# A two-block network on one core: the second mixer's gate panels and attention output projection traced in pieces among its four streams

## The chip, the core and the metric

The kernel runs on one core of a Trainium2 chip. The metric is the device time of one execution in microseconds; the smaller the better. A core has TensorE (PE in the rows, with PEld for its weight loads), VectorE (DVE), ScalarE (ACT), GpSimd (POOL) and SyncE (SP), which only issues DMAs here.

## What is computed

The reference passes a sequence of 512 positions with 1024 channels through two blocks of two layers each. The change touches only the mixer of the second block's layers:

```python
proj = rmsnorm(x, norm_mix_pre) @ w_in
q, k, v, rw, gate_a, gate_b = _split(proj, (ATT_Q, ATT_KV, ATT_KV, RW_SHIFT_COLS, D_MODEL, D_MODEL))
y_att = sliding_window_attention(rope(q), rope(k), v, att_sinks) @ w_o_att
y_rw = rwkv7_time_mix(rw, ...) @ w_o_rw
mixed = sigmoid(gate_a) * y_att + sigmoid(gate_b) * y_rw
x = x + rmsnorm(mixed @ w_out, norm_mix_post)
```

`sliding_window_attention` has 16 query heads of 64 and 4 key heads, a window of 128. `rwkv7_time_mix` is a linear recurrence of 16 heads of 64 with a 64x64 state each.

## The kernel before

Activations lie feature by position: 8 tiles of 128 features x 512 positions. A **panel** is 128 output features of a weight matrix: 8 k tiles of 128x128. Each float32 operand is split into a high and a low part (hi, lo for activations, wh, wl for weights), and each k tile takes three matmuls of 512 columns, at lines L303 to L305 (`mm_k`). `weights` loads half a panel (four k tiles, 256 KB, L286, issued on SP), copies it to wh on ACT (L287) and subtracts to get wl (L288) on the engine that `self.lo_eng` names, VectorE or GpSimd. `proj` makes a whole panel and leaves it in a PSUM bank.

`mixer2` handles the heads in 8 pairs, and has four streams.

- `keys` runs `rw_a` for each pair: the projection of the keys, small matmuls for decay and norm (L1114, L1121, L1133), elementwise work down to the tile bk (L1146, L1147), and then 8 matmuls at L1157. After every second pair `rw_solve` inverts small triangles on VectorE (L1185, L1186).
- `attention` projects keys, values and queries, rotates them (`rope2`, L943 to L947), and goes through 16 blocks of scores (L983) and values (L1012, L1023). Its result od goes to DRAM.
- `preps` runs `rw_prep`: two projections per pair, then the chunk matrices of the scan (from L1236 on, with a sum over heads at L1246).
- `seqs` runs `rw_seq`: 8 steps per pair, each with two small matmuls (L1317) and copies out of PSUM (L1319, L1320), then a normalisation (L1324 to L1333), transposes (L1339, copied out at L1344) and the gating product (L1350, L1351), whose result yd goes to DRAM.

The first two streams make the keys and attention stage, the last two the scan stage. `interleave` walks through the generators of a stage with an estimated clock, `self.now`, and so sets the order in which their instructions are **traced**. A scheduler then orders each engine's instructions by its own estimates: of what is ready, the instruction traced first goes first, and buffers are handed out in the order that results. What was traced later can thus move ahead into a gap if its buffers are free. Each engine then works strictly through its own order, and waits by semaphores.

Beside the streams there is dense work with no recurrence in it: 16 gate panels (two of them made earlier, with the head of the mixer), each followed by a Tanh on ACT (L1424) and a store, and the 8 panels of w_o_att (`att_out`) on the reloaded attention output. Each of these is multiplied by its gate at L1487 and stored as md. Before, both are traced after all four streams. Rings of buffers are named by `self.S`: gates use the weight ring wg (for the later ones wa too) and the banks mg and sc; attention scores use these two banks as well, projections of keys the bank x1, those of attention x2. `att_out` splits its input into the 16 buffers that hold the mixer's input H until the last projection. `mixer2_out`, which comes next, reloads yd and runs the panels of w_o_rw.

Of the kernel before, what the change touches and what calls it, by code (L numbers as in the profile page):

```python
# [212 lines left out]
class Builder:  # L213
# [110 lines left out]
    def proj(self, panel, acts, bank=None):  # L324
        o = self.ps(bank)
        self.mm3(o, panel, acts)
        return o

# [874 lines left out]
    def rw_prep(self, l, i, H, st):  # L1203
# [6 lines left out]
        v = self.shift(self.proj(win[28 + i], H, "x2"), *self.mu_cols(l, 16 + i))  # L1210
        yield 10.4, 1.0
# [172 lines left out]
    def interleave(self, gens, fill=()):  # L1384
# [4 lines left out]
        rest = [[self.now, g, s] for s, g in fill]  # L1389
        while live:  # L1390
            t = next((t for t in live + rest if t[0] <= self.now + 1e-9), None)
            if t is None:
                self.now = min(t[0] for t in live + rest)
                continue
            self.S = t[2]
            try:
                pe, lat = next(t[1])
                self.now += pe
                t[0] = self.now + lat
            except StopIteration:  # L1400
                (live if t in live else rest).remove(t)
# [9 lines left out]
    def mixer2(self, l, H, pre):  # L1411
# [10 lines left out]
        def gate(j):  # L1422
            t = self.T("gt")
            nc.scalar.activation(t, pre[j] if j in pre else self.proj(win[j], H), AF.Tanh, scale=0.5)  # L1424
            nc.scalar.dma_start(sga[j - 38] if j < 46 else sgb[j - 46], t)

        def gates():
            for i in range(8):
                self.S = "G" if i < self.NG else "G2"
                for j in (38 + i, 46 + i):  # L1430
                    if j not in pre:
                        gate(j)
                        yield 5.2, 0.0

        st = [dict() for _ in range(8)]
# [10 lines left out]
        for j in self.HEAD2[3:]:  # L1446
            gate(j)
        self.S = "K"
        self.rw_low(l, H, pre)
        with ExitStack() as es:  # L1450
# [8 lines left out]
            self.interleave([("K", keys((1, 2, 3))), ("A", self.attention(l, H, od, pre[9]))])  # L1459
        with ExitStack() as es:  # L1460
# [20 lines left out]
            def att_out():  # L1481
                Y = self.reload(od)
                for m in range(8):
                    g = self.T("g")
                    nc.sync.dma_start(g, sga[m])
                    o = self.proj(self.I[f"q_w_o_att{l}"][m], Y)
                    nc.vector.scalar_tensor_tensor(out=g, in0=g, scalar=1.0, in1=o, op0=ADD, op1=MUL)  # L1487
                    nc.scalar.dma_start(md[m], g)

            self.lo_eng = nc.vector  # L1490
            self.interleave([("A", seqs()), ("K", preps())])
            self.S = "G"
            for _ in gates():
                pass
            self.S = "M"
            att_out()
# [125 lines left out]
    def ple(self, l, X, pre, out):  # L1622
# [32 lines left out]
    NG = 3  # L1655
# [51 lines left out]
```

## Time and profile before

| | us |
|---|---|
| median of 3 runs | 4038.19 |
| lowest, highest | 4032.23, 4041.36 |
| the profiled execution | 4036.65 |
| its span, first to last instruction | 4034.8 |

Two layers of the second block follow each other; mixer of layer 0 lies between about 1480 and 2200 us of the span, that of layer 1 some 1297 us later. The rows further down are read like this: busy time of an engine is the time in which one of its instructions ran; a granted clock (PEclk) of 1.00 is TensorE's upper level, 2.4 GHz, and 0.5 its lower one, 1.2 GHz, so a mean between them says how much of a stretch was spent at each.

### The profile page before, as it was taken

The numbers are of one execution on the slowest core, as the hardware profiler recorded it, in microseconds if no ns is written. First come the engines' busy times: TensorE is split into PE (matmuls) and PEld (weight loads), VectorE is DVE, ScalarE is ACT, GpSimd is POOL, SyncE is SP. The second block draws the span as 40 slices with busy tenths as digits, with TensorE's granted clock in tenths as the row PEclk, the third lists the DMA queues.
The fourth block names the chain that finished last, engine by engine and source line by source line (L and its number), as shares of the span: only waits on it lengthen the run. The fifth ranks groups of instructions, "written<-read, shape, count | busy, mean of one in ns | idle before, by whom it ended". The sixth has DMA issues, their size and how long they took to land.

```text
span 4034.8 us, 56574 instructions
## 1 busy us (share of the span) xinstructions
PE 3762.3 (93%) x19888; PEld 3117.2 (77%) x19888; DVE 2667.9 (66%) x5595; ACT 1774.9 (44%) x3727; POOL 576.6 (14%) x515
## 2 busy tenths in 40 slices
PE   7998999999999988889999999998888989999998
PEld 6877888888888876657778888896665777888887
DVE  7888444555644567887664676687788775476667
ACT  4433333544433352435553554455344555354444
POOL 0201000110100033222110200014331220020001
PEclk9999999999999998989999999999888999999999
DMA  8466333312333343343227433344334323743334
GB/s 287 153 204 189 97 94 95 94 48 63 100 95 96 91 147 105 97 128 109 91 65 255 124 107 92 99 153 152 96 98 130 110 81 101 234 126 97 94 96 137
DMA packets 316573, 487.34 MB, mean 121 GB/s; under 512 B 79744, under 2 KB 127744, under 8 KB 316160
## 3 DMA queue, kind: packets, MB, share of 16 engines
q1 hardware_dynamic: 240256, 422.82, 34.0%
q10 hardware_dynamic: 76032, 60.90, 4.7%
q8 instruction: 157, 2.57, 0.3%
q14 instruction: 128, 1.05, 0.1%
HBM read 422.72 MB, written 60.88 MB: 120 GB/s over the span
## 4 chain that ended last, share of the span: by engine, by line
PE 55%; DVE 13%; ACT 3%; issue 3%; POOL 1%; DMA 1%; ACTq 0%; SPq 0%; POOLq 0%; DVEq 0%
PE ps L303 15%; PE ps L304 15%; PE ps L305 15%; DVE tm L1185 2%; PE ps L1317 1%; DVE tt L1186 1%; PE ps L1300 1%; PE ps L1157 1%; DVE ro L946 1%; DVE wl L288 1%; PE ps L983 1%; ACT wh L287 1%; PE ps L1023 1%; PE ps L1280 1%; PE ps L1285 1%
## 5 line engine op out<-in xcount | busy, mean ns | idle before, releaser
L303 PE MATMUL ps<-hi,wh 128*128 128x512 f32 (+1 forms) x4384 | 1635.3, 374 | 41.5 <-DVE ro L946 18.1
L305 PE MATMUL ps<-hi,wl 128*128 128x512 f32 (+1 forms) x4384 | 1622.1, 371 | 9.7 <-DVE wl L288 5.2
L304 PE MATMUL ps<-lo,wh 128*128 128x512 f32 (+1 forms) x4384 | 1622.7, 371 | 7.8 <-DVE lo L449 4.6
L287 ACT ACTIVATE wh<-raw 128x512 fp32r<-128x512 f32 (+1 forms) x1158 | 710.1, 620 | 1281.8 <-PE ps L304 1065.7
L288 DVE TENSOR_TENSOR wl<-raw,wh 128x512 fp32r<-128x512 f32 (+1 forms) x1005 | 690.8, 693 | 515.9 <-ACT wh L287 487.1
L303 PEld LDWEIGHTS ps<-hi,wh 128*128 128x128 f32 x4384 | 840.6, 192 | 181.3 <-issue 19.6
L305 PEld LDWEIGHTS ps<-hi,wl 128*128 128x128 f32 x4384 | 841.4, 192 | 143.7 <-DVE wl L288 7.8
L304 PEld LDWEIGHTS ps<-lo,wh 128*128 128x128 f32 x4384 | 842.5, 192 | 138.4 <-DVE lo L449 4.9
L288 POOL TENSOR_TENSOR wl<-raw,wh 128x512 fp32r<-128x512 f32 (+1 forms) x153 | 200.1, 1318 | 1193.2 <-ACT wh L287 1165.2
L1381 POOL TENSOR_TENSOR x<-x,ys 128x256 f32<-128x256 f32 x48 | 43.6, 909 | 862.9 <-DVE ys L1380 793.0
L482 DVE SCALAR_TENSOR_TENSOR ad<-ad,cact 128x1024 f32<-128x1024 f32 x96 | 116.7, 1220 | 29.2 <-DMA ad<-in_ada 29.1
L175 DVE TENSOR_TENSOR acc<-acc,sq 128x256 f32<-128x256 f32 (+1 forms) x175 | 96.1, 552 | 25.2 <-ACT sq L174 23.1
L1157 PE MATMUL ps<-bk,adg 128*128 128x192 f32 x256 | 67.2, 384 | 46.5 <-DVE bk L1147 20.5
L1319 DVE COPY sv<-ps 64x64 f32<-64x64 f32 x224 | 49.5, 221 | 90.4 <-PE ps L1317 87.6
L1185 DVE TENSOR_TENSOR tm<-lu,tt 128x126 f32<-128x126 f32 (+22 forms) x248 | 100.1, 404 | 9.0 <-DMA lu<-ls 4.0
L1580 DVE TENSOR_TENSOR u<-ps,r 128x512 f32<-128x512 f32 x88 | 60.5, 690 | 67.7 <-PE ps L305 67.0
L1317 PEld LDWEIGHTS ps<-sv,add 128*128 128x128 f32 (+1 forms) x512 | 77.9, 189 | 31.9 <-issue 8.8
L1292 POOL TENSOR_SCALAR add<-rdg 64x512 f32<-64x512 f32 x32 | 51.5, 1609 | 351.3 <-DVE add L1301 226.6
L1157 PEld LDWEIGHTS ps<-bk,adg 128*128 128x128 f32 x256 | 47.3, 216 | 64.8 <-issue 34.2
L1317 PE MATMUL ps<-sv,add 128*128 128x64 f32 (+1 forms) x512 | 91.1, 272 | 3.7 <-DVE sv L1319 2.3
L1320 ACT ACTIVATE y<-ps 64x64 f32<-64x64 f32 x256 | 54.7, 216 | 88.7 <-DVE sv L1319 49.5
L1186 DVE TENSOR_TENSOR tt<-tt,tm 128x126 f32<-128x126 f32 (+22 forms) x248 | 80.7, 325 | 3.7
(356 smaller groups left out, 5168.7 us busy)
## 6 DMA issues: line engine op xcount, KB each, us to landing
raw<-in_q_win SPq DMA_DIRECT2D x224, 256.0 KB, 2.9
ad<-in_ada SPq DMA_DIRECT2D x96, 512.0 KB, 4.4
raw<-in_q_w_up SPq DMA_DIRECT2D x184, 256.0 KB, 2.7
raw<-in_win SPq DMA_DIRECT2D x98, 256.0 KB, 3.1
raw<-in_w_val SPq DMA_DIRECT2D x92, 256.0 KB, 2.6
raw<-in_w_gate SPq DMA_DIRECT2D x92, 256.0 KB, 2.8
raw<-in_q_w_down SPq DMA_DIRECT2D x74, 256.0 KB, 2.6
raw<-in_w_down SPq DMA_DIRECT2D x64, 256.0 KB, 2.6
```

Source lines behind the costliest of these rows:

```text
L175: nc.vector.tensor_tensor(out=self.acc[:, cs], in0=self.acc[:, cs], in1=q, op=ADD)
L287: nc.scalar.activation(h, raw, AF.Copy)
L288: self.lo_eng.tensor_tensor(out=l, in0=raw, in1=h.bitcast(F32), op=SUB)
L303: nc.tensor.matmul(o, h, ah, start=k == first, stop=False)
L304: nc.tensor.matmul(o, h, al, start=False, stop=False)
L305: nc.tensor.matmul(o, l, ah, start=False, stop=k == last)
L482: nc.vector.scalar_tensor_tensor(out=raw, in0=raw, scalar=1.0, in1=self.cact, op0=MUL, op1=MUL, accum_out=m)
L1157: nc.tensor.matmul(o, ad[:, c], bk[:, c], start=True, stop=True)
L1185: nc.vector.tensor_tensor(out=t, in0=lc, in1=tt[:, 0:c, j:j + 1].to_broadcast([P, c, n]), op=MUL)
L1186: nc.vector.tensor_tensor(out=tt[:, 0:c, j + 1:32], in0=tt[:, 0:c, j + 1:32], in1=t, op=ADD)
L1317: nc.tensor.matmul(o, add[h][rows, c], c3(sv[h])[rows, c], start=True, stop=True)
L1580: nc.vector.tensor_tensor(out=u, in0=pj(ff), in1=r2, op=MUL)
```

## The change

The gates and `att_out` become one generator, `dense`, that is handed to both calls of `interleave` as `fill`. It yields after each half panel (four k tiles, 12 matmuls). `interleave` keeps a credit: each segment of a stream adds its estimated TensorE time times a share (0.27 in the keys and attention stage, 0.25 in the scan stage), and pieces are traced while the credit is above zero, or when no stream is due. What is left after the streams is traced at the end. The w_o_att part may begin only once pair 7's projections are traced (`st["proj"]`), since it needs H's buffers. While a piece is traced, `lo_eng` is GpSimd. In the first stage the pieces take the banks x2 and x1 in turn, in the second sc and mg; the ring of gate tiles (2) now also holds g of the w_o_att part. Nothing is computed differently.

```diff
+    def pieces(self, panel, acts, out):
+        o, ws = self.ps(), []
+        for k in range(len(acts)):
+            if k % self.WK == 0:
+                ws.append(self.weights(panel[:, k:min(len(acts), k + self.WK)]))
+            self.mm_k(o, ws, acts, k, slice(0, S))
+            if k % self.WK == self.WK - 1 and k < len(acts) - 1:
+                yield 0.68 * self.WK
+        out.append(o)
...
         v = self.shift(self.proj(win[28 + i], H, "x2"), *self.mu_cols(l, 16 + i))
+        st["proj"] = True
         yield 10.4, 1.0
...
+        def piece():
+            nonlocal credit
+            s, g = fill
+            self.S, lo, self.lo_eng = s, self.lo_eng, self.nc.gpsimd
+            pe = next(g, None)
+            self.lo_eng = lo
+            credit -= pe or 0.0
+            self.now += pe or 0.0
+            return pe
+
         while live:
-            t = next((t for t in live + rest if t[0] <= self.now + 1e-9), None)
+            t = next((t for t in live if t[0] <= self.now + 1e-9), None)
             if t is None:
-                self.now = min(t[0] for t in live + rest)
+                if not (fill and piece()):
+                    self.now = min(t[0] for t in live)
                 continue
...
                 t[0] = self.now + lat
+                credit += pe * share
             except StopIteration:
-                (live if t in live else rest).remove(t)
+                live.remove(t)
+            while fill and credit > 0.0 and piece():
+                pass
...
-        def gates():
+        def dense():
             for i in range(8):
-                self.S = "G" if i < self.NG else "G2"
                 for j in (38 + i, 46 + i):
                     if j not in pre:
-                        gate(j)
-                        yield 5.2, 0.0
+                        o = []
+                        yield from self.pieces(win[j], H, o)
+                        gate(j, o[0])
+                        yield 0.68 * self.WK
+            while "proj" not in st[7]:
+                yield 0.0
+            Y = self.reload(od)
+            yield 0.01
+            for m in range(8):
+                g = self.T("g")
+                nc.sync.dma_start(g, sga[m])
+                o = []
+                yield from self.pieces(self.I[f"q_w_o_att{l}"][m], Y, o)
+                nc.vector.scalar_tensor_tensor(out=g, in0=g, scalar=1.0, in1=o[0], op0=ADD, op1=MUL)
+                nc.scalar.dma_start(md[m], g)
+                yield 0.68 * self.WK
...
-            self.interleave([("K", keys((1, 2, 3))), ("A", self.attention(l, H, od, pre[9]))])
+            self.interleave([("K", keys((1, 2, 3))), ("A", self.attention(l, H, od, pre[9]))], ("F", fill), self.SHARE[0])
...
-            self.interleave([("A", seqs()), ("K", preps())])
-            self.S = "G"
-            for _ in gates():
+            self.interleave([("A", seqs()), ("K", preps())], ("F2", fill), self.SHARE[1])
+            self.S = "M"
+            for _ in fill:
                 pass
-            self.S = "M"
-            att_out()
...
+    SHARE = 0.27, 0.25
```

Three places in TensorE's order show what moves. The first is layer 0's keys stage, between the norm of pair 6 (L1133 before, L1144 after) and its first matmul at L1157 (L1168 after). Before:

```order
L1133 MATMUL ps_15362<-c_hsel,sq_15329 128x64 x4
L1023 MATMUL ps_15397<-pt_15388,vt_13534 64x256
L1023 MATMUL ps_15397<-pt_15395,vt_13534 64x256 x2
L1012 MATMUL ps_15438<-ident,sc_15257 128x128
L1012 MATMUL ps_15438<-ident,sc_15260 128x128
L1012 MATMUL ps_15438<-ident,sc_15257 128x128
L1012 MATMUL ps_15438<-ident,sc_15260 128x128
L983 MATMUL ps_15480<-kd_13546,ro_14845 128x256
L983 MATMUL ps_15480<-kd_13546,ro_14890 128x256
L1157 MATMUL ps_15450<-bk_13139,adg 128x192
```

Afterwards, with ps_15708 a gate's bank (its first rows; eight more matmuls of it, two small ones and the next projection stand before L1168):

```order
L1144 MATMUL ps_15462<-c_hsel,sq_15440 128x64 x4
L1023 MATMUL ps_15538<-ident,sc_15065 128x128
L1023 MATMUL ps_15538<-ident,sc_15062 128x128
L1023 MATMUL ps_15538<-ident,sc_15065 128x128
L303 MATMUL ps_15708<-hi_12288,wh_15710 128x512
L304 MATMUL ps_15708<-lo_12289,wh_15710 128x512
L305 MATMUL ps_15708<-hi_12288,wl_15711 128x512
```

A gate's long matmuls now stand where only attention's small ones stood. The second place is layer 0's scan stage, right after pair 7's last projection. Before, with ps_18522 a gate:

```order
L305 MATMUL ps_18011<-hi_12302,wl_18032 128x512
L1236 MATMUL ps_18120<-rdg_15778,bk_18092 128x128 x4
L1236 MATMUL ps_18129<-rdg_15778,bk_18092 128x128 x4
L304 MATMUL ps_18522<-lo_12291,wh_18524 128x512
L305 MATMUL ps_18522<-hi_12290,wl_18525 128x512
L303 MATMUL ps_18522<-hi_12292,wh_18524 128x512
```

Afterwards, with ps_18661 the first panel of w_o_att and hi_18613, lo_18614 its reloaded input:

```order
L305 MATMUL ps_18571<-hi_12302,wl_18592 128x512
L303 MATMUL ps_18661<-hi_18613,wh_18663 128x512
L304 MATMUL ps_18661<-lo_18614,wh_18663 128x512
L305 MATMUL ps_18661<-hi_18613,wl_18664 128x512
L303 MATMUL ps_18661<-hi_18619,wh_18663 128x512
L304 MATMUL ps_18661<-lo_18620,wh_18663 128x512
```

Four panels of w_o_att, 96 matmuls, now come between pair 7's projections and its scan matrices. The third place is pair 7's steps, at the end of the scan stage. Before, with ps_18642 a gate:

```order
L1317 MATMUL ps_18335<-sv_18118,add_18116 128x64
L303 MATMUL ps_18642<-hi_12294,wh_18644 128x512
L304 MATMUL ps_18642<-lo_12295,wh_18644 128x512
L305 MATMUL ps_18642<-hi_12294,wl_18645 128x512
L303 MATMUL ps_18642<-hi_12296,wh_18662 128x512
L304 MATMUL ps_18642<-lo_12297,wh_18662 128x512
L1317 MATMUL ps_18342<-sv_18118,add_18116 128x64
```

Afterwards (L1329 is the step, L1351 the transposes, L310 to L312 the gating product, ps_19454 the first panel of w_o_rw):

```order
L1329 MATMUL ps_19320<-sv_18931,add_18929 128x64
L1329 MATMUL ps_19320<-sv_18932,add_18930 128x64
L1351 MATMUL ps_19347<-ident,y_19270 64x128 x4
L1351 MATMUL ps_19354<-ident,y_19270 64x128 x4
L310 MATMUL ps_19363<-sghi_13094,hi_19364 128x512
L311 MATMUL ps_19363<-sglo_13095,hi_19364 128x512
L312 MATMUL ps_19363<-sghi_13094,lo_19365 128x512
L310 MATMUL ps_19363<-adhi_13128,hi_19364 128x512
L311 MATMUL ps_19363<-adlo_13129,hi_19364 128x512
L312 MATMUL ps_19363<-adhi_13128,lo_19365 128x512
L303 MATMUL ps_19454<-hi_19404,wh_19456 128x512
```

Pair 7's 16 step matmuls stand in one block, and no panel is left to stand between them. Layer 1's order reads alike in all three places.

## Rows read from the trace of the kernel before

**Rows 1.** The page, part 1: busy us, share of the span, instructions.
```profile
PE 3762.3 (93%) x19888; PEld 3117.2 (77%) x19888; DVE 2667.9 (66%) x5595; ACT 1774.9 (44%) x3727; POOL 576.6 (14%) x515
```
**Rows 2.** Busy us by stretches: length, PE, PEld, DVE, ACT, POOL, PEclk, DMA share, GB/s.
```profile
1490.00:1808.00 318.00, 269.82 (x1249) 196.37 (x1247) 244.18 (x639) 125.34 (x331) 98.54 (x82) 0.89 0.35 105
1808.00:2122.00 314.00, 287.55 (x1745) 229.90 (x1745) 216.76 (x502) 162.33 (x423) 59.30 (x46) 0.98 0.30 94
2122.00:2200.00 78.00, 78.00 (x344) 64.08 (x343) 32.94 (x51) 29.70 (x51) 0.00 (x0) 1.00 0.77 253
2787.00:3105.00 318.00, 269.22 (x1248) 196.05 (x1245) 247.77 (x643) 126.54 (x332) 97.65 (x82) 0.89 0.34 105
```
**Rows 3.** The same view, two slices of the keys stage and one of the tail.
```profile
1570.00:1590.00 20.00, 13.51 (x48) 10.39 (x49) 19.15 (x43) 3.10 (x5) 6.91 (x7) 0.67 0.30 85
1710.00:1730.00 20.00, 18.43 (x72) 13.14 (x70) 18.22 (x54) 8.17 (x25) 4.99 (x5) 0.59 0.34 93
2130.00:2150.00 20.00, 20.00 (x90) 16.57 (x89) 5.18 (x8) 5.97 (x11) 0.00 (x0) 1.00 0.84 284
```
**Rows 4.** Waits of PE, 1490 to 1808: line, releaser, us in total, times, longest.
```profile
PE ps L1157 <- DVE bk L1147: 10.2, 3, 5.3
PE ps L303 <- DVE ro L946: 9.0, 5, 4.8
PE ps L1157 <- DVE bk L1146: 5.6, 2, 3.5
PE ps L1157 <- DVE n L1139: 4.1, 1, 4.1
```
**Rows 5.** Timeline of PE in layer 0's keys stage: start, us, what, idle before.
```profile
1571.73 0.98 PE L1157 MATMUL ps<-bk,adg 128*128 128x192 f32 x2 [5.33 <-DVE bk L1147]
```
**Rows 6.** Waits of PE, 1808 to 2122, the longest.
```profile
PE ps L1246 <- DVE add L1243: 17.7, 7, 4.3
```
**Rows 7.** Line L1424, a gate's Tanh, by stretches: ACT busy and its instructions.
```profile
1490.00:1808.00 318.00, 0.58 (x1) 0.89 0.35 105
1808.00:2122.00 314.00, 3.52 (x6) 0.98 0.30 94
2122.00:2200.00 78.00, 4.09 (x7) 1.00 0.77 253
```
**Rows 8.** Line L1487, a panel of w_o_att taken from PSUM, in the tail.
```profile
2122.00:2200.00 78.00, 4.90 (x8) 1.00 0.77 253
```
**Rows 9.** The page, part 5: count, busy us, mean ns of one, idle before.
```profile
L288 DVE TENSOR_TENSOR wl<-raw,wh 128x512 fp32r<-128x512 f32 (+1 forms) x1005 | 690.8, 693 | 515.9 <-ACT wh L287 487.1
L288 POOL TENSOR_TENSOR wl<-raw,wh 128x512 fp32r<-128x512 f32 (+1 forms) x153 | 200.1, 1318 | 1193.2 <-ACT wh L287 1165.2
```
**Rows 10.** Timeline near 1513 (POOL, DVE), and line L1147: ns min/median/max.
```profile
1512.87 1.30 POOL L288 TENSOR_TENSOR wl<-raw,wh 128x512 fp32r<-128x512 f32 x1
1512.95 1.76 DVE L1147 TENSOR_TENSOR bk<-zs,wi 128x512 f32<-128x512 f32 x1 [3.71 <-POOL zs L1142]
...
L1147 DVE TENSOR_TENSOR bk<-zs,wi x16: 636/678/1761, 1513.0 to 3084.7; 128x512 f32<-128x512 f32 x16
```
**Rows 11.** Timeline of pair 7's steps and what follows them, layer 0.
```profile
2102.71 0.22 ACT L1320 ACTIVATE y<-ps 64x64 f32<-64x64 f32 x1
2111.50 0.55 PE L1317 MATMUL ps<-sv,add 128*128 128x64 f32 x4
2113.26 0.69 DVE L1324 TENSOR_REDUCE mn<-y 128x8 f32<-128x512 f32 x1 [0.94 <-ACT y L1320]
2116.44 0.17 DVE L1331 TENSOR_SCALAR vr<-vr 128x8 f32<-128x8 f32 x1
2118.78 0.69 DVE L1333 TENSOR_TENSOR y<-y,ry 128x512 f32<-128x512 f32 x1
2120.24 2.29 ACT L1344 ACTIVATE yf<-ps,vec 64x256 f32<-64x256 f32 x4 [2.44 <-PE ps L1339]
2123.36 0.69 DVE L1351 TENSOR_TENSOR yf<-ps,yf 128x512 f32<-128x512 f32 x1
```

More of the change, by code (lines that the diff above doesn't have):

```diff
@@ L1382, in post_half, with interleave @@
             then(m, x, cs)
-    def interleave(self, gens, fill=()):
+    def interleave(self, gens, fill=None, share=0.0):
         live = [[self.now, g, s] for s, g in gens]
-        rest = [[self.now, g, s] for s, g in fill]
+        credit = 0.0
+        def piece():
[7 more added lines that the diff above has]
+            return pe
         while live:
-            t = next((t for t in live + rest if t[0] <= self.now + 1e-9), None)
+            t = next((t for t in live if t[0] <= self.now + 1e-9), None)
             if t is None:
-                self.now = min(t[0] for t in live + rest)
+                if not (fill and piece()):
+                    self.now = min(t[0] for t in live)
                 continue
@@ L1420, in mixer2, with gate @@
         pre = dict(zip(self.HEAD2, pre))
-        def gate(j):
+        def gate(j, o):
             t = self.T("gt")
-            nc.scalar.activation(t, pre[j] if j in pre else self.proj(win[j], H), AF.Tanh, scale=0.5)
+            nc.scalar.activation(t, o, AF.Tanh, scale=0.5)
             nc.scalar.dma_start(sga[j - 38] if j < 46 else sgb[j - 46], t)
-        def gates():
+        def dense():
             for i in range(8):
-                self.S = "G" if i < self.NG else "G2"
                 for j in (38 + i, 46 + i):
                     if j not in pre:
-                        gate(j)
-                        yield 5.2, 0.0
+                        o = []
[14 more added lines that the diff above has]
+                yield 0.68 * self.WK
+        fill = dense()
         st = [dict() for _ in range(8)]
@@ L1446, in mixer2 @@
         for j in self.HEAD2[3:]:
-            gate(j)
+            gate(j, pre[j])
         self.S = "K"
@@ L1479, in seqs @@
                     yield from self.rw_seq(l, i, st[i])
[L1481 to L1488, printed above, removed]
             self.lo_eng = nc.vector
-            self.interleave([("A", seqs()), ("K", preps())])
-            self.S = "G"
-            for _ in gates():
-                pass
-            self.S = "M"
-            att_out()
+            self.interleave([("A", seqs()), ("K", preps())], ("F2", fill), self.SHARE[1])
+            self.S = "M"
+            for _ in fill:
+                pass
         return sgb, md
@@ L1653, in ple @@
         return dst, H, nxt.banks if l == 0 else None
-    NG = 3
+    SHARE = 0.27, 0.25
     HEAD2 = (36, 37, 9, 38, 46)
```

6 rows, old and new, of the table RINGS2 are left out of this document.

## The prediction, made before the changed kernel was timed

> **What bounds the kernel now.** I read the page first: PE is busy for 93% of the span [rows 1], so on the whole TensorE sets the time, and a change that moves no work off PE can only win where PE stands still or runs slowly. The change touches one stretch per layer of the second block, the mixer, so the next view is the busy time by stretches [rows 2]. Layer 0's mixer falls into three stages. In the keys and attention stage (1490 to 1808 us) PE is busy 269.82 of 318 us, at a granted clock of 0.89, and DVE 244.18. In the scan stage (1808 to 2122) PE is busy 287.55 of 314 at clock 0.98. In the dense tail (2122 to 2200) PE is busy 78.00 of 78 at clock 1.00, and DVE and ACT well under half. Layer 1 repeats this 1297 us later; its keys stage shows PE at 269.22 [rows 2], so I work out one layer and double it.
>
> So the tail is bound by PE alone, while PE idles 318 - 269.8 = 48.2 us in the keys stage and 314 - 287.6 = 26.4 us in the scan stage. The clock adds to that: a mean of 0.89 instead of 1.00 over 318 us is worth at most 0.11 x 318 = 35 us. The low stretches are those where PE has few matmuls, as 1570 to 1590 (0.67, DVE busy 19.15 of 20) and 1710 to 1730 (0.59) [rows 3]. The room in the keys stage is thus 48 + 35 = 83 us a layer. What ends PE's idle time there is mostly DVE [rows 4]: bk of the keys (L1147 and L1146, 15.8 us together), the rotary copies at L946 (9.0) and the norms of the keys (L1139, 4.1). In the scan stage one wait stands out: L1246 for DVE's add L1243, 17.7 us in 7 times [rows 6].
>
> **The change, part by part, for one layer.** The unit is one panel: 8 k tiles of 3 matmuls of 512 columns. In dense PE work 90 of these take 20.00 us [rows 3], 0.222 us each, so 24 take 5.33 us. No matmul is added; they move. Before, one gate's Tanh (beside the two of the head) ran in the keys stage, 6 in the scan stage and 7 in the tail, and all 8 products with w_o_att in the tail [rows 7, 8]. Counted in PE's order, the keys stage goes from 27 gate matmuls to 252, so +225 x 0.222 = 50.0 us; the scan stage gets +111 (24.6 us); the tail loses 336 (74.6 us). These sum to zero, so the change in time is: new idle time minus idle time and slow clock recovered.
>
> (a) *Recovered in the keys stage.* All 50.0 us could vanish in a room of 83 us; that is the upper end. The lower end is below nothing, since PE takes its queue in order and the gates stand ahead of matmuls that DVE waits for. The order gives a middle. Waits at L1157 for these DVE lines make 19.9 us in 6 times [rows 4]. In the new order only pairs 4 and 6 get ten or more gate matmuls in front of L1157; pair 2, with the longest wait (5.33 us at 1566, [rows 5]), gets none. The waits for L946 are better covered, since a projection of the keys now stands in front. I take a third of the idle time, 16 us, and 40% of the clock loss, 14 us, since the gates bring long matmuls evenly into the stage: 30 us. This is a choice between -5 and 50, nearer to the upper end because DVE (244 of 318 us busy) gets no gate work in this stage.
>
> (b) *Recovered in the scan stage.* Gates still stand in pairs 0 and 1, one of whose waits at L1246 is the longest (4.3 us) [rows 6]; pairs 2 to 6 have none, before or after. I take 5 us, between 0 and 9.
>
> (c) *New: the reload of the attention output.* It now follows pair 7's projections directly, into buffers that these have just read. Eight splits are needed, each an ACT copy and a DVE subtraction; the nearest row is the weight split of the same shape, 0.693 us on DVE [rows 9]. PE's first panel waits for the last six: 4.2 us of DVE, with 18 other DVE operations among them in the order, of 0.17 to 0.69 us [rows 11], some 6 us more. PE has 23 matmuls meanwhile, 5.1 us, and so waits about 5 us (0 to 10). Before, this lay under gates in the tail.
>
> (d) *New: the end of the scan is bare.* In the new order nothing but pair 7's own work stands between the last w_o_att panel and the first panel of w_o_rw. The trace gives the length: pair 7's steps from 2102.71 on, the normalisation on DVE from 2113.26 to 2119.47, four ACT copies of 2.29 us together from 2120.24, the last DVE operation to 2124.05, then a split (0.69) [rows 9, 11]. That is 22 us, of which two weight splits (1.2) belong to gates: 21 us. PE's useful work there is 12 matmuls at 0.222 and about 24 small ones at 0.14 (four in 0.55) [rows 11], 6 us, so 15 us are new idle time. Before, gates lay under it and panels of w_o_att behind it. After it the clock must come back: 20 us at 0.59 or 0.67 [rows 3] cost 7 to 8 us at full use, so I take 4. Together 19 us, between 12 and 25.
>
> The cause of (d) also shows in the order: 96 matmuls of w_o_att (21 us) now stand between pair 7's last projection and its first scan matmul, so fewer panels are left to cover what follows.
>
> (e) *POOL.* All 22 moved panels now split their weights on POOL: 44 of about 1.3 us (the mean is 1.318) instead of DVE's 0.693 [rows 9]. POOL has room (98.54 of 318 and 59.30 of 314 busy, [rows 2]). PE waits for POOL only where the split is late; I take 0 and keep the rest for a rival. The moved weight loads keep their count and SP's queue carries a third of DMA time in these stages against 0.77 in the tail [rows 2], so they cost nothing. The moved Tanh and store issues sit on ACT, 125 of 318 us busy.
>
> Sum for a layer: -30 - 5 + 5 + 19 = -11 us, for two -22 us. The profiled execution took 4036.65 us (its span is 4034.8), 1.5 under the median of 4038.19. So 4014.7 for such an execution and 4016 as a median.
>
> **Rivals.** *The gates vanish in the keys stage* (faster by more). DVE paces the stage and all 50 us fit in the room of 83: -50 - 5 + 24 = -31 a layer, 3976. For it: DVE 18 to 19 of 20 us busy where PE is slowest [rows 3]. Against it: the waits at L1157 that nothing new covers.
>
> *A wash.* The keys stage gives back 15 to 23 us, as much as (c) and (d) cost; the time stays within 8 us, 0.2%, which is about what a measurement can tell from no change. For it: the uncovered waits, and PE in order.
>
> *Slower: the gates delay the chain.* The gates now take turns in the same two PSUM banks (x1, x2) as the projections of keys and attention, which have one buffer each, so a projection cannot start until the gate in its bank is finished and evacuated, and DVE then gets its keys 5.3 us later. If that happens for most gates the keys stage gives back 5 us only: -5 - 5 + 24 = +14 a layer, 4066. It decides from the point where the keys stage returns less than 19 us a layer; under 15 the loss can be measured. Against it: in the order other matmuls mostly stand between a gate's end and the next projection.
>
> *Slower: POOL holds up DVE.* The trace shows a DVE operation with two SBUF inputs that took 1.76 us instead of 0.678 while a weight split ran on POOL [rows 10], 1.08 us lost. 22 more splits in the keys stage at 1.08 are 24 us of DVE, bringing it to 268 of 318; if 20 of these reach the path, the stage returns 10: -10 - 5 + 24 = +9 a layer, 4056. Against it: many of DVE's operations there read PSUM, and splits also meet an idle DVE. The Trainium skill, "SBUF — State Buffer", section "SBUF: two separate sides", speaks against this change: DVE operations with two SBUF inputs and GpSimd operations take turns on an exclusive port pair, and the one that comes second waits for the whole of the other. By that rule DVE would lose up to a full POOL operation for each split that it meets; the trace's row agrees in kind.
>
> *The pieces stay together.* The scheduler could have put the panels back in the tail; the order excludes that.
>
> **How the numbers follow.** Forecast (-4 to -22 a layer) 0.40; gates vanish 0.18; wash 0.17; bank delay 0.17; POOL 0.08. So faster 0.58, same 0.17, slower 0.25, and 4016 as the likeliest. Each layer's terms go from -50 - 9 + 12 to +5 + 35, too wide for 8 in 10; I leave out half of the fastest rival below 3974 and half of the bank delay above 4066.
>
> **What would show it.** The span from the first L1157 to the first scan matmul should grow by about 20 us a layer in place of 50, with a clock above 0.89; no dense tail should be left after pair 7's last step; PE should show about 21 us of low use ahead of the first w_o_rw panel and a low clock behind it; the wait of L304 for the split at L278 should appear ahead of the first w_o_att panel. The forecast is wrong if the keys stage grows by 35 us or more, if PE waits long for POOL's splits, or if panels of w_o_rw start under pair 7's steps.

## The result, and the profile after

The changed kernel takes 4068.19 us (median of 4 runs, 4053.68 to 4072.16) against 4038.61 for the kernel before beside it: ratio 1.0069, 95% interval 1.0042 to 1.0096, slower by 0.7%. The forecast was 4016 (3974 to 4066); the sign was wrong, and the time lies just outside the range. The profiled execution took 4067.77 us, its span is 4065.7. Lines of the changed kernel are shifted: L946 is now L957, L1157 is L1168, L1147 is L1158, L1246 is L1258, L1185 and L1186 are L1196 and L1197.

The page's part 1 answers to [rows 1]; GpSimd alone has more to do, 88 operations and 122 us:

```profile
PE 3774.0 (93%) x19888; PEld 3127.0 (77%) x19888; DVE 2666.3 (66%) x5507; ACT 1780.7 (44%) x3727; POOL 698.4 (17%) x603
```

The busy time by stretches for layer 0, columns as in [rows 2] (length, PE, PEld, DVE, ACT, POOL, granted clock, DMA share, GB/s): the keys stage, the scan stage up to pair 7's last step, and the 12 us after it.

```profile
1490.00:1852.00 362.00, 314.78 (x1479) 234.97 (x1477) 275.08 (x671) 144.25 (x363) 132.70 (x106) 0.94 0.38 117
1852.00:2202.00 350.00, 316.83 (x1845) 254.44 (x1845) 214.22 (x465) 171.81 (x434) 85.43 (x66) 0.96 0.35 107
2202.00:2214.00 12.00, 5.59 (x16) 3.30 (x16) 5.13 (x15) 4.32 (x9) 0.00 (x0) 0.50 0.00 0
```

The keys stage had 318 us with 48.2 of PE idle; now it has 362 with 362 - 314.78 = 47.2. Matmuls came in, the clock rose from 0.89 to 0.94, and the idle time stayed. Its waits have changed places, as PE's waits from 1488 to 1852 show against [rows 4]: less at L1168 (once L1157), more for the rotary copies.

```profile
PE ps L303 <- DVE ro L957: 19.5, 6, 4.8
PE ps L1168 <- DVE n L1149: 6.8, 2, 4.5
PE ps L1168 <- DVE bk L1158: 3.6, 1, 3.6
```

For all that follows a layer is cut at two marks read from the trace: the **keys stage** runs from the first Tanh of a head gate to the first matmul of the scan, the **rest** from there to the first panel of w_out taken from PSUM.

| us, layer 0 / layer 1 | keys stage | rest |
|---|---|---|
| before | 323.8 / 324.3 | 441.1 / 441.1 |
| after | 364.9 / 368.6 | 413.6 / 410.6 |
| change | +41.1 / +44.3 | -27.5 / -30.5 |
| the same without the 50.0 us of matmuls moved in or out | -9 / -6 | +22 / +20 |

So a layer loses about 14 us. The rest costs in sum what was forecast: -5 + 5 + 19 = +19. The keys stage does not: it gives back 9 and 6 us, not 30.

### The profile page after: what moved, and what is told of

It is laid out like the page before. It is cut to its first block, busy times and chain, and to the rows that moved or that the text cites. A ratio compares the mean times of both kernels' runs of the same rounds, so it can differ in the third digit from the quotient of the medians.

```text
span 4065.7 us, 56468 instructions
## 1 busy us (share of the span) xinstructions
PE 3774.0 (93%) x19888; PEld 3127.0 (77%) x19888; DVE 2666.3 (66%) x5507; ACT 1780.7 (44%) x3727; POOL 698.4 (17%) x603
## 5 line engine op out<-in xcount | busy, mean ns | idle before, releaser
L303 PE MATMUL ps<-hi,wh 128*128 128x512 f32 (+1 forms) x4384 | 1644.1, 376 | 53.8 <-DVE ro L957 39.1
L305 PE MATMUL ps<-hi,wl 128*128 128x512 f32 (+1 forms) x4384 | 1627.4, 372 | 17.6 <-DVE wl L288 10.6
L303 PEld LDWEIGHTS ps<-hi,wh 128*128 128x128 f32 x4384 | 843.7, 193 | 201.0 <-issue 30.3
L288 DVE TENSOR_TENSOR wl<-raw,wh 128x512 fp32r<-128x512 f32 (+1 forms) x917 | 628.8, 692 | 471.0 <-ACT wh L287 454.9
L288 POOL TENSOR_TENSOR wl<-raw,wh 128x512 fp32r<-128x512 f32 (+1 forms) x241 | 315.5, 1319 | 1446.2 <-ACT wh L287 1352.4
L1329 PEld LDWEIGHTS ps<-sv,add 128*128 128x128 f32 (+1 forms) x512 | 82.1, 203 | 43.8 <-ACT y L1332 23.6
L1329 PE MATMUL ps<-sv,add 128*128 128x64 f32 (+1 forms) x512 | 97.7, 290 | 16.3 <-ACT y L1332 10.8
L1196 DVE TENSOR_TENSOR tm<-lu,tt 128x126 f32<-128x126 f32 (+22 forms) x248 | 108.1, 436 | 4.9
L1197 DVE TENSOR_TENSOR tt<-tt,tm 128x126 f32<-128x126 f32 (+22 forms) x248 | 95.3, 384 | 5.6
L1007 ACT ACTIVATE sc<-sc,am 128x256 f32<-128x256 f32 (+1 forms) x128 | 60.1, 471 | 68.3 <-DVE am L1003 62.8
L1168 PE MATMUL ps<-bk,adg 128*128 128x192 f32 x256 | 66.6, 367 | 20.7 <-DVE n L1149 11.7
```

Of the source, the lines that this page charges most:

```text
L288: self.lo_eng.tensor_tensor(out=l, in0=raw, in1=h.bitcast(F32), op=SUB)
L303: nc.tensor.matmul(o, h, ah, start=k == first, stop=False)
L305: nc.tensor.matmul(o, l, ah, start=False, stop=k == last)
L1168: nc.tensor.matmul(o, ad[:, c], bk[:, c], start=True, stop=True)
L1196: nc.vector.tensor_tensor(out=t, in0=lc, in1=tt[:, 0:c, j:j + 1].to_broadcast([P, c, n]), op=MUL)
L1197: nc.vector.tensor_tensor(out=tt[:, 0:c, j + 1:32], in0=tt[:, 0:c, j + 1:32], in1=t, op=ADD)
```

## The experiments

Times are medians; the ratio is to the kernel before in the same series of runs. In one execution, two layers of one kernel whose matmuls stand in nearly the same order in the trace (97% of the lines match in sequence) still differ by up to 9 us in this stage (352.8 and 344.5, 366.8 and 357.8 below), so single stages are read to some 9 us and smaller effects by the times.

| kernel | gate matmuls in keys stage, layer 0 (before: 27) | keys stage | rest | time | ratio |
|---|---|---|---|---|---|
| e1_bank_mg | 252 | 363.4 / 367.5 | 414 / 415 | 4075.0 | 1.0095 [1.0078, 1.0112] |
| e2_vector_split | 252 | 352.7 / 373.0 | 412 / 415 | 4066.3 | 1.0070 [1.0055, 1.0085] |
| e3_hold_four | 252 | 365.9 / 365.0 | 416 / 414 | 4069.0 | 1.0067 [1.0052, 1.0082] |
| e5_no_keys_fill | 60 | 333.8 / 335.1 | 434 / 434 | 4042.5 | 1.0010 [1.0001, 1.0019] |
| e6_no_split | 252 | 352.7 / 358.3 | 414 / 411 | 4046.7 | 1.0022 [1.0011, 1.0032] |
| e7_quarter_matmuls | a quarter | 364.2 / 368.1 | 412 / 410 | 4060.9 | 1.0057 [1.0037, 1.0077] |
| e8_attention_first | 336 | 423.5 / 420.8 | 403 / 402 | 4158.8 | 1.0290 [1.0273, 1.0307] |
| e10_order_alone | a quarter | 340.0 / 343.2 | 414 / 415 | 4018.2 | 0.9940 [0.9920, 0.9960] |
| e11_no_lows | a quarter | 344.6 / 347.5 | 412 / 414 | 4027.5 | 0.9963 [0.9947, 0.9979] |
| e12_no_copies | a quarter | 366.8 / 357.8 | 413 / 411 | 4053.7 | 1.0028 [1.0013, 1.0044] |
| e13_loads_only | a quarter | 352.8 / 344.5 | 413 / 413 | 4021.9 | 0.9952 [0.9934, 0.9970] |
| e14_keys_fill_only | 252 | 365.8 / 359.6 | 412 / 408 | 4061.5 | 1.0053 [1.0036, 1.0070] |
| e16_no_lows_all | 252 | 357.7 / 363.9 | 411 / 412 | 4054.6 | 1.0034 [1.0021, 1.0047] |
| e17_double_lows | 252 | 391.8 / 399.1 | 411 / 413 | 4129.5 | 1.0222 [1.0205, 1.0238] |
| e15_small_share | 144 | 324.5 / 341.6 | 411 / 411 | 4001.3 | 0.9903 [0.9886, 0.9919] |
| e18_small_share_pool | 144 | 341.6 / 337.0 | 411 / 418 | 4018.7 | 0.9941 [0.9926, 0.9956] |
| e19_full_share_vector | 252 | 350.5 / 350.8 | 414 / 410 | 4038.1 | 0.9996 [0.9986, 1.0005] |
| e20_share_018 | 192 | 334.4 / 353.6 | 413 / 410 | 4023.2 | 0.9966 [0.9955, 0.9977] |

A quarter means 81 or 82 matmuls, since nearly all of the 14 gates then run in the stage. In layer 1 the traces show 12 long matmuls less in the stage for e14 and e19, 23 less for e18 and 28 less for e20; they run in the rest.

### The forecast's own rivals: banks, and the engine of the low parts

e1 gives the pieces of the keys stage another PSUM bank:

```diff
-"F": ["x2", "x1"]
+"F": ["mg"]
```

> The fill of the keys and attention stage takes the bank mg (shared with the attention scores) in place of x2 and x1 (shared with the projections). Stage length from the head's first gate Tanh to the first scan matmul, layer 0: 323.8 us in the kernel before, 364.9 in the changed kernel. Theory of the banks (gates hold up the projections through x1 and x2): about 345 us, and PE's wait of L303 for the rotary copies (19.5 us in the changed kernel, 9.0 before) back to about 9; total about 4028. Theory of POOL (its splits slow DVE) and theory of the queue (the gates' matmuls themselves stand ahead of what the chain waits for): 360 to 370 us, total 4060 to 4075.

e2 makes the low parts of all pieces on VectorE:

```diff
-            self.S, lo, self.lo_eng = s, self.lo_eng, self.nc.gpsimd
+            self.S, lo, self.lo_eng = s, self.lo_eng, self.nc.vector
```

> The weights of the fill are split on DVE in place of POOL, in both stages. Theory of POOL: the keys stage falls from 364.9 to about 345 us, total about 4030. Theories of the banks and of the queue: the stage stays or grows, 365 to 380 us, since DVE gets 22 more splits of 0.69 us (15 us); total 4065 to 4090.

The banks x1 and x2 fall: keys stage and time did not come down. The wait of L303 for the rotary copies did, to 10.6 us, but others took its place (7.4 us at L1132). What sharing mg with the scores costs, e1 does not tell apart. e2's time did not move either, and I first took that as the end of the GpSimd rival. It was not: layer 0 of e2 was 12 us shorter, and layer 1 longer. The matmuls of its layer 1 stand in another order than in its layer 0 (in time order about half of their lines match; 89% do between its layer 0 and the changed kernel's). The scheduler had answered the edit with a new order in one layer, and that hid the effect.

### What in a piece costs: matmuls, loads, copies, low parts

e6 uses the first gate's weights for all gates of the keys stage, so nothing is loaded or split for them. e7 keeps the preparation and makes 6 of 24 matmuls. e10 does both. The rest of this group keeps e7's quarter of the matmuls: e11 leaves out only the low parts, e12 only ACT's copies, e13 both.

```diff
+            if k == 0 and self.S == "F" and self.kept:
+                ws = self.kept
...
+            if self.S != "F" or k in (0, len(acts) - 1):
+                self.mm_k(o, ws, acts, k, slice(0, S))
```

> In the keys stage all gates use the weights of the first one, which is loaded and split once (so the gates' values differ): 20 splits less on POOL and 20 copies less on ACT, with all matmuls kept. Theory of POOL: the keys stage falls from 364.9 us to about 340. Theories of the banks and of the queue: 355 to 368 us.

> In the keys stage each gate makes 6 of its 24 matmuls (k tiles 0 and 7), so the gates' values differ; loads, splits, Tanh and banks stay. Theory of the queue: of the 41 us by which the stage grew, three quarters go, 330 to 340 us. Theory of POOL: 355 to 365 us. Theory of the banks: between, 345 to 355 us, since a bank is held for a shorter time but still taken in turn.

> In the keys stage each gate's panel makes only 6 of its 24 matmuls, and with weights loaded and split once for all: neither the matmuls (as in the run with a quarter of them, 364.2 us) nor the preparation of the weights (as in the run without it, 352.7 us) is left, only the trace order. If the preparation of the weights is what delays the streams, the stage falls to 325 to 335 us; if the order in which the streams were put is the cause, it stays at 345 to 360; if the two earlier runs were long for different reasons, matmuls in the one and preparation in the other, it falls to 325 to 335 too, and the run with the order kept tells.

> A quarter of the gates' matmuls in the keys stage, as in the run that took 364.2 and 368.1 us up to the first scan matmul; weights are loaded and copied to the high part, and the low parts of the first gate are used again, so GpSimd makes no splits for these gates (values differ). Without any preparation the same stage took 340.0 and 343.2 us. If GpSimd's splits are what the preparation costs (its operations against VectorE's, or PE waiting on them), the stage falls to 340 to 348; if ACT's copies or the loads are, it stays at 358 to 368.

> The same with loads and GpSimd's low parts kept (from the first gate's high parts), and no copies on ACT for these gates (values differ). If the copies that stand in ACT's queue ahead of the streams' own work are what the preparation costs, the stage falls from 364 and 368 us to 340 to 348; if the splits on GpSimd are, it stays at 358 to 368; if each does a part, both runs lie at 346 to 358.

> The same with the loads alone, neither copies nor low parts for these gates (values differ). If the loads (DMA and SyncE's queue) cost nothing, the stage is that of the run without any preparation, 338 to 345 us; if they carry the delay, 355 to 368.

e7 was the surprise: with 170 matmuls less in the stage (38 us of PE) it is as long as in the changed kernel (what is left stands in another order; some 56% of the lines match). With the preparation there, PE's queue thus does not seem to set its length. e10 shows that the preparation does: without it the stage falls by 24 and 25 us. Of the preparation, the low parts carry most: leaving them out (e11) gives 20 and 21 us; leaving out the copies (e12) gives -3 and +10, within the spread; e13 has neither, and against e10 the loads cost 13 and 1, in an execution that took 8 us more than e13's median. The times are clearer: of the 43 us from e7 to e10 the low parts are 33, the copies 6 (e11 to e13), the loads 4. e12 against e13 is the sharpest pair, since 95% of the lines of their orders match: 18 operations more on GpSimd, 14 and 13 us more. Busy time in the keys stage of layer 0 (columns as above), e13 and then e12:

```profile
1485.00:1837.00 352.00, 299.66 (x1328) 218.23 (x1326) 267.28 (x670) 134.47 (x348) 112.53 (x91) 0.88 0.41 122
```

```profile
1491.00:1858.00 367.00, 307.68 (x1332) 221.37 (x1330) 277.88 (x671) 135.59 (x349) 135.93 (x109) 0.87 0.39 118
```

POOL's 23.4 us more go with 10.6 us more of DVE at the same count of its operations. With all matmuls there (e6) the preparation is worth 12 and 10 us, less than the 24 and 25 with a quarter of them; matmuls and splits seem in part to wait out each other, which no run tests by itself, and e6's order matches the changed kernel's to two thirds only. e11 came out as expected if the splits cost; e6, e10 and e13 fell between the ranges of their rivals in at least one layer. (The run with the order kept, which e10's text speaks of, was not made.)

### Do the low parts cost in the changed kernel as it stands?

e16 has all matmuls, loads and copies and only no low parts for these gates; e17 makes each low part twice.

```diff
-        self.lo_eng.tensor_tensor(out=l, in0=raw, in1=h.bitcast(F32), op=SUB)
+        for _ in range(2 if self.S == "F" else 1):
+            self.lo_eng.tensor_tensor(out=l, in0=raw, in1=h.bitcast(F32), op=SUB)
```

> The changed kernel with all matmuls, loads and copies of the keys stage's gates, only without the low parts made on GpSimd for them (the first gate's are used again; values differ). TensorE's order in the keys stage is nearly that of the changed kernel. If GpSimd's splits delay the stage by holding up VectorE, the stage falls from 364.9 and 368.6 us to 350 to 356 and VectorE's operations are some 15 us shorter in sum; the time is 4040 to 4050. If their cost shows only where matmuls are few, the stage stays at 362 to 369.

> The changed kernel, with each low part of the keys stage's gates made twice on GpSimd (the same result, about 24 more operations of 1.3 us a layer). PE hardly waits for these splits in the trace. If they hold up VectorE, its operations grow by another 10 to 15 us in sum and the stage from 365 and 369 us to 373 to 390; 4085 to 4120 in all. If GpSimd's work runs beside VectorE's, the time stays within 8 us of 4068.

Yes: 4054.6, 4068.2 and 4129.5 us with none (but the first gate's), one and two. e16 came out smaller than expected, its stage 7 and 5 us shorter, and e17 larger, 27 and 31 us longer. The busy time of layer 0's keys stage (columns as above) in e16, after and e17 in this order:

```profile
1490.00:1848.00 358.00, 313.11 (x1504) 234.17 (x1504) 266.26 (x680) 145.91 (x366) 113.89 (x92) 0.95 0.39 121
```

```profile
1488.00:1852.00 364.00, 316.78 (x1495) 236.97 (x1494) 277.05 (x672) 144.85 (x365) 134.70 (x108) 0.94 0.39 118
```

```profile
1488.00:1880.00 392.00, 330.48 (x1501) 244.34 (x1501) 298.40 (x680) 146.02 (x366) 159.83 (x128) 0.90 0.36 110
```

POOL goes from 113.9 over 134.7 to 159.8 us. DVE, which has nothing new to do (680, 672 and 680 operations), goes from 266.3 over 277.1 to 298.4: each step on GpSimd makes VectorE's own operations longer. Two other ways for the splits to cost are small. TensorE's order is nearly the same (94 and 91% of the lines match the changed kernel's in e16, 92 and 89% in e17). And the streams hardly wait longer for GpSimd's own share of their work: in layer 0 VectorE's waits for GpSimd come to 8.5, 8.5 and 7.4 us, TensorE's to 4.4, 4.4 and 8.6. Which operations of VectorE grow, the groups of DVE in that stage tell (line, shapes, count, busy us, mean ns, idle before). e16:

```profile
L1003 DVE TENSOR_TENSOR sc<-ps,band 128x512 f32<-128x512 f32 x24 | 16.3, 685 | 16.3 <-PE ps L1027 8.6 <-PE ps L998 7.6
...
L1016 DVE TENSOR_SCALAR sc<-sc,am 128x256 f32<-128x256 f32 x48 | 14.1, 346 | 0.2
```

The same two groups in after and in e17:

```profile
L1012 DVE TENSOR_SCALAR sc<-sc,am 128x256 f32<-128x256 f32 x48 | 18.3, 434 | 0.2
L999 DVE TENSOR_TENSOR sc<-ps,band 128x512 f32<-128x512 f32 x24 | 16.3, 684 | 14.3 <-PE ps L994 7.6 <-PE ps L1023 6.7
```

```profile
L1013 DVE TENSOR_SCALAR sc<-sc,am 128x256 f32<-128x256 f32 x48 | 21.6, 498 | 0.2
L1000 DVE TENSOR_TENSOR sc<-ps,band 128x512 f32<-128x512 f32 x24 | 16.3, 684 | 18.8 <-PE ps L1024 12.3 <-PE ps L995 6.3
```

The operation on the scores that reads and writes SBUF goes from 346 over 434 to 498 ns; the one that reads PSUM stays at 685, 684, 684. One place of e17, DVE and then POOL (start, us, operations run together), shows how:

```profile
1755.06 4.24 DVE L1013 TENSOR_SCALAR sc<-sc,am 128x256 f32<-128x256 f32 x4
```

```profile
1755.22 5.24 POOL L289 TENSOR_TENSOR wl<-raw,wh 128x512 fp32r<-128x512 f32 x4 [3.03 <-ACT wh L287]
```

Four operations of VectorE that take 346 ns each on average in e16 (1.4 us in all) take 4.24 us, the last three 1.37 to 1.39 us each, beside four of GpSimd of 1.3 us: the two engines go in step.

### The other places: attention's turn, the end of the scan, the share

e3 holds the last four panels of w_o_att until all streams are through. e5 hands no fill to the keys stage. e8 lists attention ahead of the keys. e14 hands the fill to the keys stage alone; the rest is traced behind the streams, as before.

```diff
+                while m >= 4 and not self.scanned:
+                    yield 0.0
```

> The last four panels of w_o_att may be traced only once all four streams of the layer are through; 40 of their matmuls then stand under pair 7's steps. If the bare end of the scan (26.8 us from the last w_o_att matmul to the first of w_o_rw, about 23 us of cost a layer) is a loss of its own, some 9 us of matmuls fill it and the rest of the panels run behind it as they did before: 10 to 20 us a layer less, 4030 to 4048 in all. If the end was only where PE would have waited anyway, the time stays at 4068.

> No fill is handed to the keys stage; the gates go into the scan stage, and 105 matmuls of w_o_att are left under pair 7's steps. If the gates in the keys stage are what delays it (364.9 us instead of 323.8 up to the first scan matmul), that stretch is back at 322 to 330 us. The scan stage then has 396 dense matmuls more than before under its steps: if they hide as badly as in pairs 0 to 2 (which returned nothing) the time is that of before less the covered end, 4025 to 4040; if the steps hide them, 4000 to 4025. If the keys stage is as long as with the gates, the cause lies elsewhere.

> Attention's stream is listed ahead of the keys' in the keys stage; the gates are there as in the changed kernel. In its trace attention's last block came 56 us later than before (349 us after the stage's start against 293), the keys' last bk only 20 us later (323 against 303). If the stage is long because the pieces push attention behind the keys, it shrinks from 364.9 to 330 to 350 us and the time to 4010 to 4045. If the pieces delay both streams by their own work, the stage stays within 10 us of 365 and the time within 4055 to 4075.

> The fill is handed to the keys stage alone; what is left of the gates and all of w_o_att are traced after the four streams, as before. The keys stage should be that of the changed kernel (365 to 369 us, some 9 us a layer less than the work that it took over), and the dense tail behind the steps is back, so the last pair's steps are bare (59 gate matmuls stood under them before, 13 us) but the normalisation and the reload behind them are covered. If the bare end costs what its terms say, 4025 to 4045; if the loss of the changed kernel is the keys stage's alone, 4055 to 4070.

e3 moved the bare end without shortening it: 40 matmuls stand between pair 7's first step and its transposes, and none are left behind them. Its busy time just after the steps, with the clock at its lower level:

```profile
2200.00:2210.00 10.00, 3.22 (x6) 1.66 (x6) 3.87 (x6) 1.14 (x3) 0.00 (x0) 0.50 0.71 250
2210.00:2220.00 10.00, 4.72 (x11) 3.47 (x12) 4.74 (x7) 4.42 (x7) 0.00 (x0) 0.51 1.05 397
```

e5 brings the keys stage near that of before and the time to 4042.5, 0.1% above that of before: the scan stage hides nothing, but it takes nothing either, as long as the tail's work also serves as cover. (Its stage still grew by 10 and 11 us with 33 more gate matmuls, which the scheduler pulled in.) e8 speaks against the idea that the stage is long because attention is starved: the 29th of the 32 copies of its result out of PSUM then comes at 242 us of the stage (349 in the changed kernel, 293 before), but the keys' chain is left for the end, and the stage is 59 and 52 us longer, with 84 more gate matmuls (19 us) in it. e14 costs nearly as much as the changed kernel although w_o_att stands behind the steps again: with 252 gate matmuls made early, none is left between pair 7's first step and its transposes, where 59 stood before (33 of them among the steps). The number is the one that was expected if the loss were the keys stage's alone, but the trace shows the bare end again: TensorE waits 6.03 us for the normalised y, as in the changed kernel, so w_o_att did not cover it.

```profile
2166.36 1.89 PE L1351 MATMUL ps<-ident,y 128*64 128x128 f32 x8 [6.03 <-DVE y L1345]
```

e15 therefore makes fewer gates early (share 0.13), puts the low parts on VectorE, and keeps e14's tail. e18 is e15 with the low parts on GpSimd, e19 is e15 with share 0.27, e20 with 0.18.

```diff
-    SHARE = 0.27, 0.25
+    SHARE = 0.13, 0.25
...
-            self.S, lo, self.lo_eng = s, self.lo_eng, self.nc.gpsimd
+            self.S, lo, self.lo_eng = s, self.lo_eng, self.nc.vector
...
-            self.interleave([("A", seqs()), ("K", preps())], ("F2", fill), self.SHARE[1])
-            self.S = "M"
+            self.interleave([("A", seqs()), ("K", preps())])
+            self.S = "F2"
```

> A version made to beat both: share 0.13 in the keys stage (144 gate matmuls there instead of 252), low parts on VectorE, and all other dense work traced behind the streams as before, so that 63 gate matmuls stand under pair 7's steps again and the products with w_o_att behind them. The keys stage takes over 117 matmuls, 26 us. If it gives back a third of that, as from no fill to all of it with VectorE's splits, 9 us a layer: 4020 to 4030. If VectorE pays for the splits in full: 4036 to 4050.

> The version with share 0.13 and the dense tail behind the streams (4001.3 us, keys stage 324.5 and 341.6), but with the low parts of the pieces on GpSimd as in the changed kernel. If the amount of gates in the stage decides, and not the engine of the low parts, the time stays within 8 us of 4001. If GpSimd's splits decide, the stage grows by some 8 to 12 us a layer (half as many splits as in the changed kernel): 4015 to 4028.

> Share 0.27 again (252 gate matmuls in the keys stage), low parts of the pieces on VectorE, the dense tail behind the streams. With GpSimd's low parts this took 4061.5 us. If the engine decides, 4015 to 4035; if the share decides because VectorE has then no room for the splits either, 4045 to 4062.

> Between the two: share 0.18, 192 gate matmuls in the keys stage, low parts on VectorE, 54 gate matmuls left under pair 7's steps. If the stage hides what its idle time and clock leave room for, the 48 further matmuls (11 us a layer) cost nothing and the time is 3980 to 3998; if its room is used up at 144, they return nothing: 4001 to 4020.

| time, us | low parts on GpSimd | on VectorE |
|---|---|---|
| share 0.27 | 4061.5 (e14) | 4038.1 (e19) |
| share 0.13 | 4018.7 (e18) | 4001.3 (e15) |

e15 was faster than expected and e18 as expected for GpSimd's splits; e19 fell between its two ranges, e20 above both of its own. Both count, and nearly add: the engine is worth 23 and 17 us, the share 43 and 37. The 17 us lie in layer 0: there e18 and e15 match to 96% in order and keys stage and rest together differ by 17 us, in layer 1, matching as well, by 2 to 3. What a split costs thus depends on what it meets. e15 is faster than both kernels, by 1.0% (0.8 to 1.1%) against the kernel before. Its layer 0, keys stage, scan up to pair 7, its steps, and 111 us behind them:

```profile
1485.00:1809.00 324.00, 288.41 (x1392) 213.61 (x1391) 255.63 (x655) 137.47 (x352) 101.56 (x83) 0.95 0.38 114
1809.00:2096.00 287.00, 261.67 (x1630) 210.04 (x1628) 207.09 (x470) 152.76 (x393) 59.36 (x47) 0.98 0.31 98
2096.00:2109.00 13.00, 13.00 (x70) 9.73 (x68) 6.31 (x20) 6.35 (x21) 0.00 (x0) 1.00 0.23 82
2109.00:2220.00 111.00, 110.70 (x490) 90.65 (x490) 56.76 (x95) 42.21 (x72) 12.87 (x8) 1.00 0.70 237
```

The same stage in e18, with 256.22 us of VectorE although some 10 of its operations went to GpSimd:

```profile
1487.00:1828.00 341.00, 300.00 (x1390) 222.30 (x1388) 256.22 (x644) 137.92 (x352) 116.09 (x93) 0.91 0.36 110
```

In e15 the stage takes in 117 matmuls (26 us) and is as long as before, 324.5 us, with PE idle for 35.6 us; steps and tail are full. Layer 1 gets another order from the scheduler (some 42% of the lines match) and takes 341.6. With 192 gate matmuls (e20) layer 0's stage is 10 us longer for 11 us of matmuls, so next to nothing more is hidden; layer 1's is 12 us longer with only 24 more in it, in yet another order. Nor does the rest shrink any further: it falls from 441 to 411 us with e15's 117 matmuls gone and stays at 414 and 410 in e19, where 24 us more have left it, since the end of the scan is then bare. So in layer 0 what is moved beyond e15's matmuls costs about its full length (keys stage and rest take 29 us more in e19, for 24 us of matmuls), in layer 1 8 of 21 us.

## Why the prediction was wrong, point by point

**(e), POOL at 0, is the step that failed first.** It asked whether PE waits for GpSimd's splits; PE hardly does; in layer 1 of the changed kernel, where the rows show it, once:

```profile
PE ps L305 <- POOL wl L288: 2.0, 1, 2.0
```

What it left out of the sum is that GpSimd holds up VectorE, through which both streams run. The forecast had it as a rival, at 0.08, with [rows 10] as its sign. With the low parts on VectorE (e19) the stage returns 50 - 26.7 = 23 us in layer 0 and 21 in layer 1, where 12 matmuls less were moved; with GpSimd (e14) 8 and 12. So (e) was worth 9 to 15 us a layer by these two, and 5 to 7 by the changed kernel against e16. The rest of the 21 and 24 us by which 9 and 6 fall short of 30 is (a)'s. The rival's arithmetic was not exact either: it forecast 24 us of VectorE's time, and e16 against after shows 277.05 - 266.26 = 10.8, yet the stage returned 9 and 6 where the rival said 10. By the Trainium skill, "SBUF — State Buffer", section "SBUF: two separate sides", the port pair that VectorE and GpSimd share is locked for a whole instruction; the lockstep above agrees, 1.3 us at a time.

**(a), 30 us returned, was too high even without GpSimd's splits**, by 7 to 9 us, since e19 returns 23 and 21 (by e16, which returns 16 and 10, by more). The room of 83 us was counted from idle time and clock, but VectorE was busy 250 of 324 us, and the streams' chains run over it. e7 shows that best: less PE work, same time. Without the low parts the same matmuls, 38 us, cost 13 and 16 us (e16 against e11, in another order too). The first 117 matmuls found room in layer 0 (e15: 25 us of 26 returned; 9 in layer 1), the next 48 next to none (e20). A share of the room was taken as returned, where the question was at which amount the return ends. "DVE gets no gate work" was true of its instructions, not of its time.

**(b) to (d) together were right:** +19 forecast, +22 and +20 measured. That the sum fits so well is in part luck, since single terms were off. (b)'s 5 us did not come. Up to pair 7's first step TensorE stood idle for 25.9 us before and for 29.5 afterwards, at granted clocks of 0.98 and 0.97 (columns as above):

```profile
1808.00:2101.00 293.00, 267.07 (x1641) 213.92 (x1641) 205.14 (x467) 152.29 (x395) 59.30 (x46) 0.98 0.30 92
1852.00:2191.00 339.00, 309.50 (x1815) 248.35 (x1815) 210.08 (x449) 168.41 (x419) 85.43 (x66) 0.97 0.35 107
```

(c) was 1.2 us of waiting, not 5:

```profile
PE ps L304 <- DVE lo L278: 1.2, 2, 0.6
```

(d) is seen where it was expected: from the first matmul behind those of w_o_att (2187.24) to the first of w_o_rw (2214.03) 26.8 us pass, not 21. Of these 3.7 are pair 6's transposes and gating product, which lie ahead of the stretch that the forecast measured, and some 2.2 are what pair 7's, the same matmuls, take longer at the granted clock of 0.50 than pair 6's; the wait for the normalised y is 6.0:

```profile
2208.62 1.89 PE L1351 MATMUL ps<-ident,y 128*64 128x128 f32 x8 [6.03 <-DVE y L1345]
```

The gates under the steps had cost next to nothing: before, 33 gate matmuls (7.3 us) stood among pair 7's steps and these took 12.1 us; now they have none and take 11.7.

**The rivals.** The bank delay decides, as said, from a return under 19 us; the return was under 19, but not through the banks (e1). "The gates vanish" is what layer 0 of e15 shows, for half of the gates. The signs put down beforehand did their work: the keys stage grew by more than 35 us, and the forecast was wrong by its own test; the clock above 0.89, the missing tail and the low clock behind the steps came as written.

What stays open: how much of the stage's growth in the changed kernel is the order that the scheduler found. e10, with neither the preparation nor three quarters of the matmuls, is still 16 and 19 us longer than before, for 12 us of matmuls. e15's two layers, with the same work and some 42% of the order in common, differ by 17 us; e16 returns 16 and 10 us with no low parts but the first gate's, less than e19 with them on VectorE. And the stage grows by more than VectorE's own lengthening (e17: +27 us for +21). The rows of e17 show where TensorE spent it: with as many matmuls it was busy for 13.7 us more, at a granted clock of 0.90 instead of 0.94, and idle for 14.3 us more; which delays led to that was not shown.

## What to carry to other kernels

Idle TensorE time inside a latency chain is room only for as much filler as the chain's own engine leaves alone; count what a filler does to that engine, and find the amount at which it stops being hidden (here, in layer 0, between 117 and 165 added matmuls) instead of moving everything. Keep as much independent work for the end as the last serial steps need for cover. Where a scheduler sets the order, compare the order of both layers before an unchanged time is read as "no effect".

## What the runs showed of the hardware

GpSimd's subtraction of two 128x512 SBUF tiles (1.3 us) holds up not only VectorE's operations with two SBUF inputs but also one with one tensor and a scalar column (346 ns on average in e16, up to 1.45 us in the changed kernel). Doubling these operations, 25 us of POOL in layer 0's stage, where VectorE waited 7.4 us and TensorE 8.6 us for POOL in all, made the stage 27 and 31 us longer: GpSimd's time was paid about one for one. And moving this work to VectorE, where the same subtraction takes 0.69 us on average, was cheaper than leaving it on the idle-looking engine, by 23 us (e19 against e14) and 17 us (e15 against e18); in e2 a new order in one layer hid the gain.
